# Where one block sum is made: GpSimd in place of VectorE for product 7 of a seven-product matmul group

## The chip, the core and the metric

One core of a Trainium2 chip runs the whole program. The metric is device time in microseconds (us) for one execution: the kernel before took 1982.58 us in the median of 3 runs (1981.91 to 1983.2).

## The reference, cut to what matters

One decoder layer on 256 tokens of width 2048, in float32: a half-step SwiGLU feed-forward, a two-branch attention mixer, and a second half-step feed-forward, with layer norms between them.

```python
def _swiglu(x, w_gate, w_up, w_down):
    return (jax.nn.silu(x @ w_gate) * (x @ w_up)) @ w_down
...
h = _layer_norm(ALPHA * h + 0.5 * _swiglu(h, ffn1...), ...)
mix = _mixer(h, positions, w_in, ...)          # gates, q/k/v projections, attention, w_out
h = _layer_norm(ALPHA * h + mix, ...)
h = _layer_norm(ALPHA * h + 0.5 * _swiglu(h, ffn2...), ...)
```

The change touches matmuls of the 256 x 2048 activations by weight columns: gate and up of both feed-forwards (2048 x 5632 each), and gates and differential-attention projections of the mixer.

## The kernel before, in words

**A product of two float32 numbers in three matmuls.** Every operand is split into a rounded part and a rest. `split` (L148 to L150) makes the rounded part with a cast on ScalarE (ACT in the profile, L149) and the rest with a subtraction on VectorE (DVE, L150). `triple` (L201 to L204) then issues three matmuls on TensorE (PE): high by high (L202), high by low (L203), low by high (L204). So the two weight halves of a pair are first needed one matmul apart.

**Units and their ring.** Work on the weights goes in units of one 128x1024 tile: `load` starts a DMA on SyncE's queue, `prep` casts and subtracts into a pair of tiles from a ring (`wring`, six pairs in the groups), `now` issues the matmuls. `look(3, 4)` keeps three loaded and four prepared units ahead of the matmuls. The framework then lays out each engine's queue by priority and by when it takes an operand to be ready, so an instruction can stand earlier in its engine's queue than in the code; each engine works through its queue in order.

**A group (`Hybrid.group`, L310).** Two 512-column blocks of weights are multiplied together. For part of the depth, seven products of sums and differences stand in for eight plain ones; the rest is done plainly (`plain`, L361). The sums on the weights' side are made in place in `seventh.prep` (L341 to L347), one per half `s`: for product 5, block 11 becomes 11+12; for 6 it becomes 11+12+22; for 7, block 12 becomes 12+22; for 4, block 11 takes 21. All of these are the additions of L344. They read and write the raw weight tiles (`sraw`), which the loads of the next group overwrite when the last reader is done.

```python
plan = {1: ("11", "11", None, "X"), 5: ("12", "11", ("11", "12"), "Z"), 6: ("22", "11", ("11", "22"), "X"),
        7: (None, "12", ("12", "22"), "X"), 2: ("21", "21", None, "Y"), 4: (None, "11", ("11", "21"), "W"),
        3: (None, "22", None, "Z")}
```

The order of units is 1, 1, plain, 5, 5, plain, 6, 6, plain, 7, 7, plain and so on to product 3, with one plain unit more at the end: 14 units of six matmuls and 8 of twelve, 180 matmuls. After products 1, 5, 6 and 7 ScalarE copies a bank (L321, L322).

**Where groups run.** Each feed-forward runs ten groups (L772), the mixer six (L1011, L1020, L1026): 26 groups. A feed-forward group ends in `sum_done` (L726): VectorE adds bank and copy (`gus`, L728), ScalarE takes the silu (L715), VectorE multiplies (`hb`, L719) and transposes (`blocks`, L606), and GpSimd issues eight DMAs that store the transposed tile (`hT`, L608). In the groups GpSimd (POOL) has only such DMA issues to do.

Of the kernel before, what the change touches and what calls it, by code (L numbers as in the profile page):

```python
# [15 lines left out]
ALU = mybir.AluOpType  # L16
# [43 lines left out]
def layer_kernel(ctx: ExitStack, tc: tile.TileContext, a: dict, out: bass.AP):  # L60
    nc = tc.nc
    V, S, GP, PE = nc.vector, nc.scalar, nc.gpsimd, nc.tensor
# [9 lines left out]
    def nm(s):  # L72
        uid[0] += 1
        return f"{s}_{uid[0]}"
# [10 lines left out]
    def mm_bank(name="mm"):  # L85
        return psum.tile([P, 512], F32, tag="mm", name=nm(name), bufs=5)
# [61 lines left out]
    def split(hi, lo, src):  # L148
        S.copy(hi, src)  # L149
        V.tensor_tensor(out=lo, in0=src, in1=hi.bitcast(F32), op=ALU.subtract)  # L150
# [12 lines left out]
    def catch_up(n):  # L163
        while len(behind) > n:
            behind.popleft()()
# [22 lines left out]
    def unit(load, prep, now, later_on=None):  # L188
        if load is not None:
            load()  # L190
        loaded.append((prep, now, later_on))
        advance(*ahead)

    def next_pair():
        assert len(ring) > len(prepared) + lag[0], (len(ring), len(prepared), lag[0])
        catch_up(len(ring) - 1)
        pair = ring.pop(0)
        ring.append(pair)
        return pair

    def triple(o, xh, xl, wh, wl, first, last, again=False):  # L201
        PE.matmul(o, xh, wh, start=first, stop=False, skip_group_check=again)  # L202
        PE.matmul(o, xh, wl, start=False, stop=False, skip_group_check=again)  # L203
        PE.matmul(o, xl, wh, start=False, stop=last, skip_group_check=again)  # L204
# [93 lines left out]
    class Hybrid:  # L298
# [11 lines left out]
        def group(self, w0, w1, done):  # L310
            banks = {}
            snap = [t[:, i, :] for t in self.snaps[self.turn % len(self.snaps)] for i in range(2)]
            self.turn += 1
            n1, n2, n3, q5 = snap
            R = self.raws
            blocks = {"11": (w0, 0), "12": (w1, 0), "21": (w0, 2), "22": (w1, 2)}
# [4 lines that stand above are left out]
            after = {1: lambda: S.copy(n1, banks["X"]), 6: lambda: S.copy(n2, banks["X"]),  # L321
                     7: lambda: S.copy(n3, banks["X"]), 5: lambda: S.copy(q5, banks["Z"]),  # L322
                     2: lambda: done(0, 0, banks["Y"], n1, ALU.subtract),
                     4: lambda: done(0, 1, banks["W"], n3, ALU.subtract)}
            stops = {1, 5, 6, 7, 2, 4}

            def bank(n):
                first = n not in banks
                if first:
                    banks[n] = mm_bank()  # L330
                return banks[n], first

            def seventh(p, s):
                load_block, src, add, b = plan[p]
                st = {}

                def load():
                    w, j0 = blocks[load_block]
                    nc.sync.dma_start(R[load_block][s], w[j0 + s])

                def prep():  # L341
                    t = R[src][s]
                    if add is not None:
                        V.tensor_tensor(out=t, in0=t, in1=R[add[1]][s], op=ALU.add)  # L344
                    pair = next_pair()
                    split(*pair, t)
                    st["pair"] = [v.rearrange("p (g n) -> p g n", g=G) for v in pair]  # L347

                def now():
                    o, first = bank(b)  # L350
                    wh, wl = st["pair"]
                    xh, xl = self.seven.at_[p]
                    for g in range(G):
                        k = 2 * s + g
                        triple(o, xh[:, k, :], xl[:, k, :], wh[:, g, :], wl[:, g, :], first and g == 0,
                               s == 1 and g == 1 and p in stops, b in "XZ")
                    if s == 1 and p in after:
                        after[p]()
                unit(load if load_block else None, prep, now)

            def plain(n, j, last=False):  # L361
                w = (w0, w1)[n]
                names = (("Y", "W"), ("Z", "X"))[n]
                st = {}

                def load():
                    st["raw"] = wpool.tile([P, 1024], F32, tag="raw", name=nm("raw"), bufs=4)
                    nc.sync.dma_start(st["raw"], w[j])

                def prep():  # L370
                    pair = next_pair()
                    split(*pair, st["raw"])
                    st["pair"] = [v.rearrange("p (g n) -> p g n", g=G) for v in pair]

                def now():
                    wh, wl = st["pair"]
                    for b in range(2):
                        o, first = bank(names[b])
                        for g in range(G):
                            k = 2 * j + g  # L380
                            triple(o, self.x.at(0, k, b), self.x.at(1, k, b), wh[:, g, :], wl[:, g, :],
                                   first and g == 0, last and g == 1, n == 1)
                    if last:
                        done(1, 0, banks["Z"], n2, ALU.add)
                        done(1, 1, banks["X"], q5, ALU.add)
                unit(load, prep, now)

            end = self.k_tiles // G - 1
            for p, n, j in zip((1, 5, 6, 7) + self.last, (0, 0, 0, 0, 1, 1, 1), (4, 5, 6, 7, 4, 5, 6)):
                for s in range(2):  # L390
                    seventh(p, s)
                plain(n, j)
            plain(1, end, True)
# [927 lines left out]
```

## Time and profile before

| what | time |
|---|---|
| median of 3 runs | 1982.58 us (1981.91 to 1983.2) |
| the profiled execution: span from its first to its last instruction | 1981.9 us |
| TensorE busy in it | 1967.9 us (99%) |
| VectorE busy | 1770.4 us (89%) |
| ScalarE busy | 1247.6 us (63%) |
| GpSimd busy | 248.8 us (13%) |

Of the profiled execution the record gives the span and no time beside it. The median is 0.7 us above that span, which is as much as can lie around it. A row of the timeline gives start and length of an instruction; consecutive ones of a line are merged (x3). On VectorE the next instruction starts some 0.08 us before the one ahead of it has ended, so what an instruction costs its engine is the distance from start to start.

### The profile page before, as it was taken

The page shows a single profiled execution, that of the slowest core. Times are in us where ns is not written, and L with a number is a line of the kernel's source. Part 1 is how long each engine was busy: PE and PEld are TensorE (multiplying, and loading weights), DVE is VectorE, ACT ScalarE, POOL GpSimd, SP SyncE. Part 2 cuts the span into 40 slices and gives each one's busy share as a digit, 9 for nine tenths or more (in the row PEclk, how much of TensorE's full clock was granted, in tenths as well). Part 3 has the DMA queues.
Part 4 walks back from the last instruction along what each step waited for, and adds up shares of the span by engine and source line. Part 5 has one row for each costly group of instructions (what it writes and reads, how often), then busy time and mean ns, then how long its engine had stood idle before and what let it go on. Part 6 is the DMA issues. An engine that isn't in the chain of part 4 may idle for free.

```text
span 1981.9 us, 25344 instructions
## 1 busy us (share of the span) xinstructions
PE 1967.9 (99%) x8832; PEld 1628.9 (82%) x8832; DVE 1770.4 (89%) x2089; ACT 1247.6 (63%) x1571; POOL 248.8 (13%) x463
## 2 busy tenths in 40 slices
PE   9999999999999999999999999999999999999997
PEld 7888888888888888888888888888888888888886
DVE  7999999999799889999877676799999999998986
ACT  6666666666556566666667764566666666665552
POOL 0111101012010011002223130001011100121000
PEclk9999999999999999999999999999999999999999
DMA  8667766658678666677667667657676666596763
GB/s 323 220 212 237 262 211 202 218 199 313 232 228 274 204 221 246 220 245 250 228 215 249 228 225 264 220 208 242 225 257 229 201 216 228 186 327 225 256 222 125
DMA packets 133649, 460.50 MB, mean 232 GB/s; under 512 B 19424, under 2 KB 19472, under 8 KB 133520
## 3 DMA queue, kind: packets, MB, share of 16 engines
q1 hardware_dynamic: 109296, 389.59, 57.4%
q0 software_dynamic: 24224, 69.29, 11.2%
q8 instruction: 69, 1.13, 0.2%
q14 instruction: 60, 0.49, 0.1%
HBM read 429.97 MB, written 28.84 MB: 231 GB/s over the span
## 4 chain that ended last, share of the span: by engine, by line
PE 90%; DVE 4%; DMA 3%; issue 2%; ACT 1%; SPq 0%; POOL 0%; DVEq 0%; ACTq 0%; POOLq 0%
PE mm L203 29%; PE mm L204 29%; PE mm L202 29%; DVE wring L150 2%; DMA raw<-in_dn_dram 1%; PE tr L203 1%; PE tr L204 1%; PE tr L202 1%; ACT wring L149 1%; DVE sraw L344 0%; PE tr L571 0%; DMA hraw<-hT 0%; DMA raw<-in_wgd_dram 0%; DMA raw<-in_gu_dram 0%; DVE sraw L519 0%
## 5 line engine op out<-in xcount | busy, mean ns | idle before, releaser
L149 ACT CAST wring<-raw 128x1024 fp32r<-128x1024 f32 (+2 forms) x499 | 516.2, 1039 | 338.7 <-PE mm L204 236.6
L150 DVE TENSOR_TENSOR wring<-raw,wring 128x1024 fp32r<-128x1024 f32 (+2 forms) x499 | 596.7, 1202 | 117.0 <-ACT wring L149 110.3
L149 ACT CAST wring<-sraw 128x1024 fp32r<-128x1024 f32 x436 | 453.7, 1052 | 217.4 <-PE mm L204 98.1
L150 DVE TENSOR_TENSOR wring<-sraw,wring 128x1024 fp32r<-128x1024 f32 x436 | 523.6, 1217 | 35.2 <-ACT wring L149 31.0
L204 PE MATMUL mm<-wring,h 128*128 128x512 f32 (+2 forms) x1296 | 499.3, 386 | 0.0
L203 PE MATMUL mm<-wring,h 128*128 128x512 f32 (+2 forms) x1296 | 498.5, 385 | 0.3 <-DVE wring L150 0.3
L202 PE MATMUL mm<-wring,h 128*128 128x512 f32 (+2 forms) x1296 | 498.6, 385 | 0.0
L203 PE MATMUL mm<-wring,xs 128*128 128x512 f32 x776 | 302.3, 390 | 0.3 <-DVE wring L150 0.3
L202 PE MATMUL mm<-wring,xs 128*128 128x512 f32 x776 | 302.5, 390 | 0.0
L204 PE MATMUL mm<-wring,xs 128*128 128x512 f32 x776 | 302.1, 389 | 0.0
L204 PEld LDWEIGHTS mm<-wring,h 128*128 128x128 f32 x1296 | 243.5, 188 | 48.9 <-DVE h L150 1.4
L202 PEld LDWEIGHTS mm<-wring,h 128*128 128x128 f32 x1296 | 243.5, 188 | 48.8 <-ACT h L149 1.0
L203 PEld LDWEIGHTS mm<-wring,h 128*128 128x128 f32 x1296 | 243.5, 188 | 48.7 <-DVE wring L150 0.9
L344 DVE TENSOR_TENSOR sraw<-sraw,sraw 128x1024 f32<-128x1024 f32 x208 | 249.9, 1211 | 1.6 <-DMA sraw<-in_gu_dram 1.5
L608 POOL DMA_DIRECT2D hT<-blocks x176 | 95.7, 551 | 766.5 <-DVE blocks L606 711.5
L203 PEld LDWEIGHTS mm<-wring,xs 128*128 128x128 f32 x776 | 145.7, 188 | 31.5 <-DVE wring L150 1.6
L202 PEld LDWEIGHTS mm<-wring,xs 128*128 128x128 f32 x776 | 145.7, 188 | 31.1 <-ACT snap L321 0.7
L204 PEld LDWEIGHTS mm<-wring,xs 128*128 128x128 f32 x776 | 145.7, 188 | 30.1
L203 PE MATMUL mm<-wring,x 128*128 128x512 f32 x384 | 149.6, 390 | 0.6 <-DVE wring L150 0.6
L202 PE MATMUL mm<-wring,x 128*128 128x512 f32 x384 | 149.5, 390 | 0.3 <-ACT wring L149 0.3
L204 PE MATMUL mm<-wring,x 128*128 128x512 f32 x384 | 149.3, 389 | 0.0
L203 PEld LDWEIGHTS mm<-wring,x 128*128 128x128 f32 x384 | 72.1, 188 | 16.2 <-DVE wring L150 1.3
(268 smaller groups left out, 1921.2 us busy)
## 6 DMA issues: line engine op xcount, KB each, us to landing
raw<-in_gu_dram SPq DMA_DIRECT2D x191, 512.0 KB, 4.4
sraw<-in_gu_dram SPq DMA_DIRECT2D x160, 512.0 KB, 5.2
raw<-in_dn_dram SPq DMA_DIRECT2D x140, 512.0 KB, 4.6
sraw<-in_dn_dram SPq DMA_DIRECT2D x36, 512.0 KB, 5.3
hraw<-hT POOLq DMA_DIRECT2D x68, 256.0 KB, 5.7
raw<-in_w_out_dram SPq DMA_DIRECT2D x32, 512.0 KB, 4.4
raw<-in_wgd_dram SPq DMA_DIRECT2D x24, 512.0 KB, 4.6
hT<-blocks POOLq DMA_DIRECT2D x176, 64.0 KB, 2.3
```

The costliest lines, as they stand in the source:

```text
L149: S.copy(hi, src)
L150: V.tensor_tensor(out=lo, in0=src, in1=hi.bitcast(F32), op=ALU.subtract)
L202: PE.matmul(o, xh, wh, start=first, stop=False, skip_group_check=again)
L203: PE.matmul(o, xh, wl, start=False, stop=False, skip_group_check=again)
L204: PE.matmul(o, xl, wh, start=False, stop=last, skip_group_check=again)
L344: V.tensor_tensor(out=t, in0=t, in1=R[add[1]][s], op=ALU.add)
L608: nc.gpsimd.dma_start(to.rearrange("(g r) (i f) -> i r g f", g=4, i=4)[i], t[32 * i:32 * (i + 1), :].rearrange("r (g f) -> r g f", g=4))
```

## The change

In `seventh.prep`, the addition for product 7 is no longer issued on VectorE. When product 6 of the same half is prepared, GpSimd is given the same addition, 12 += 22, behind VectorE's addition for product 6. Product 7's cast and subtraction then read the tile that GpSimd wrote. Tiles, loads, matmuls and all other additions stay as they are.

```diff
@@ -340,8 +340,10 @@
 
                 def prep():
                     t = R[src][s]
-                    if add is not None:
+                    if add is not None and p != 7:
                         V.tensor_tensor(out=t, in0=t, in1=R[add[1]][s], op=ALU.add)
+                    if p == 6:
+                        GP.tensor_tensor(out=R["12"][s], in0=R["12"][s], in1=R["22"][s], op=ALU.add)
                     pair = next_pair()
                     split(*pair, t)
                     st["pair"] = [v.rearrange("p (g n) -> p g n", g=G) for v in pair]
```

## The prediction

> **What bounds the kernel now.** I read the page first, then who waited for whom on TensorE, then busy time by stretches of one group's length, then the timeline of one group on VectorE, TensorE and GpSimd.
>
> ```profile
> span 1981.9 us, 25344 instructions
> PE 1967.9 (99%) x8832; PEld 1628.9 (82%) x8832; DVE 1770.4 (89%) x2089; ACT 1247.6 (63%) x1571; POOL 248.8 (13%) x463
> PE 90%; DVE 4%; DMA 3%; issue 2%; ACT 1%; SPq 0%; POOL 0%; DVEq 0%; ACTq 0%; POOLq 0%
> ```
>
> TensorE is busy for 99% of the span and makes up 90% of the chain that ends last. Its waits in the whole run are these:
>
> ```profile
> PE mm L203 <- DVE wring L150: 1.2, 4, 0.4
> PE tr L98 <- DVE zero L96: 1.1, 1, 1.1
> PE tr L203 <- DVE wring L150: 0.3, 1, 0.3
> PE mm L202 <- ACT wring L149: 0.3, 1, 0.3
> ```
>
> The columns are total us, times, longest. TensorE waited for prepared weights for 1.2 + 0.3 + 0.3 = 1.8 us in all. So nothing that relieves VectorE can be worth more than about **1.8 us**, under 0.1%. But VectorE is not far from becoming the bound itself. By stretches of a group's length (for each engine busy us and instructions; then clock, DMA share, GB/s), two in the feed-forwards and the six in the mixer:
>
> ```profile
> 255.90:296.70 40.80, 40.80 (x181) 33.78 (x180) 39.55 (x41) 26.39 (x31) 4.35 (x8) 1.00 0.65 219
> 1617.40:1658.20 40.80, 40.80 (x181) 33.79 (x181) 39.54 (x41) 26.38 (x31) 4.33 (x8) 1.00 0.65 219
> 746.00:787.00 41.00, 40.89 (x182) 33.09 (x182) 39.32 (x56) 25.50 (x33) 5.45 (x10) 1.00 0.73 256
> 787.00:828.00 41.00, 40.70 (x180) 33.30 (x179) 38.07 (x36) 24.82 (x26) 2.17 (x4) 1.00 0.63 222
> 828.00:869.00 41.00, 41.00 (x183) 33.95 (x182) 38.55 (x36) 24.81 (x26) 2.16 (x4) 1.00 0.69 233
> 869.00:910.00 41.00, 41.00 (x183) 33.95 (x182) 37.46 (x37) 24.70 (x26) 5.26 (x10) 1.00 0.71 234
> 910.00:951.00 41.00, 41.00 (x183) 33.95 (x182) 38.32 (x38) 26.25 (x30) 10.10 (x20) 1.00 0.78 248
> 951.00:992.00 41.00, 41.00 (x181) 33.66 (x180) 37.15 (x37) 27.90 (x34) 9.80 (x18) 1.00 0.69 226
> ```
>
> A feed-forward group takes 40.80 us, all of it TensorE at a granted clock of 1.00; VectorE, the third pair of numbers, is busy for 39.55 of them. Its spare time is **1.25 us a group**. In the mixer it has 1.7 to 3.9. GpSimd, the fifth pair, is nearly free.
>
> **What is removed.** The timeline of VectorE in the group whose matmuls begin at 255.90:
>
> ```profile
> 248.22 1.22 DVE L344 TENSOR_TENSOR sraw<-sraw,sraw 128x1024 f32<-128x1024 f32 x1
> 249.36 1.21 DVE L150 TENSOR_TENSOR wring<-sraw,wring 128x1024 fp32r<-128x1024 f32 x1
> ...
> 253.90 1.22 DVE L344 TENSOR_TENSOR sraw<-sraw,sraw 128x1024 f32<-128x1024 f32 x1
> 255.03 0.68 DVE L728 TENSOR_TENSOR gus<-mm,snap 128x512 f32<-128x512 f32 x1
> 255.63 1.21 DVE L150 TENSOR_TENSOR wring<-sraw,wring 128x1024 fp32r<-128x1024 f32 x1
> ...
> 263.83 3.49 DVE L150 TENSOR_TENSOR wring<-sraw,wring 128x1024 fp32r<-128x1024 f32 x3
> 267.23 1.22 DVE L344 TENSOR_TENSOR sraw<-sraw,sraw 128x1024 f32<-128x1024 f32 x1
> ...
> 269.50 3.54 DVE L150 TENSOR_TENSOR wring<-sraw,wring 128x1024 fp32r<-128x1024 f32 x3
> ```
>
> Of the eight additions of L344 in the group, I take those at 253.90 and 267.23 for the two halves of product 7, by their place in the queue: the one at 248.22 is product 5's first. From start to start such an addition costs VectorE 249.36 - 248.22 = 1.14 us. Two go per group, 52 in 26 groups: 52 x 1.14 = 59 us of VectorE. On the path they are worth at most the 1.8 us above, because TensorE hides them; I count nothing.
>
> **What is added: the length of one sum on GpSimd.** The trace has no GpSimd addition. Its nearest rows:
>
> ```profile
> L608 POOL DMA_DIRECT2D hT<-blocks x176 | 95.7, 551 | 766.5 <-DVE blocks L606 711.5 <-DVE hb L719 52.5 <-issue 2.5
> L842 POOL TENSOR_SCALAR_AFFINE_SELECT mask<-mask 128x128 f32<-128x128 f32 x2 | 0.5, 287 | 0.0
> L840 POOL MEMSET mask<- 128x384 f32 x1 | 0.4, 422 | 0.0
> masks.py:197 POOL MEMSET ident<- 128x128 f32 x1 | 0.2, 204 | 0.3 <-POOLq L1305 0.3
> ```
>
> From below: the fill, which only writes, costs (422 - 204) / 256 = 0.85 ns an element, so 1024 take some 1.0 us. From above: the select reads one input and writes, 287 ns for 128 elements; eight of that size are 2.30 us, and if each of two inputs cost that much, 4.6. I take **2.3 us**, since the select is the nearest row and its start-up, counted eight times there, leaves room for the second input. [...]
>
> **What it takes from VectorE.** This is the unknown that decides. Call it b: the time by which one GpSimd sum holds VectorE up. No row shows GpSimd reading a tile while VectorE works; its DMA issues beside VectorE (0.55 us each) read none. So b lies between 0 (they run side by side) and 4.6 (VectorE stands still for the longest sum). I take b = 2.3, the whole length of one sum, for this reason: both engines would stream whole tiles at once, and between ends that far apart it is the middle and the one length that a row gives. [...]
>
> **What is queued behind it.** GpSimd's sum needs blocks 12 and 22 loaded and product 5's addition of the same half done. In the shown group VectorE made the sum at 253.90 without a wait, and product 5's first addition ended at 248.22 + 1.22 = 249.44, so GpSimd can start the first between 249.4 and 253.9, the second soon after. Behind VectorE's held instruction stand the subtractions for products 5, 6 and 7, and behind those TensorE:
>
> ```profile
> 266.79 0.39 PE L202 MATMUL mm<-wring,xs 128*128 128x512 f32 x1
> 267.02 0.39 PE L203 MATMUL mm<-wring,xs 128*128 128x512 f32 x1
> ...
> 273.59 0.39 PE L202 MATMUL mm<-wring,xs 128*128 128x512 f32 x1
> 273.82 0.39 PE L203 MATMUL mm<-wring,xs 128*128 128x512 f32 x1
> ```
>
> The L203 at 267.02 is the first to need product 6's subtraction, the first of the three at 263.83, done at 265.05: a margin of 1.97 us. The one at 273.82 needs the second half of product 7, the middle one of the three from 269.50, done at about 271.86: again 1.96. Three readings of the loss per feed-forward group, with b = 2.3:
>
> - Both sums ahead of product 6's subtraction: 2 x 2.3, less the one addition removed ahead of it (1.14), less the margin: 4.6 - 1.14 - 1.97 = 1.49.
> - Only one ahead of it: no loss there (2.3 - 3.11 is negative); at product 7, with two additions gone, 4.6 - 2.28 - 1.96 = 0.36.
> - VectorE's budget over the whole group: 39.55 - 2.28 + 4.6 = 41.87, which is 1.07 over TensorE's 40.80.
>
> I take the last, which lies between the other two and is what a steady run of groups cannot escape: 20 groups x 1.07 = 21.4 us. In the mixer the same budget adds 2.32 to 39.32, 38.07, 38.55, 37.46, 38.32 and 37.15 against 41.0; only the first exceeds it, by 0.64. Sum: **22.0 us**. On the profiled execution's span that is 1981.9 + 22.0 = 2003.9; the median of the runs is 0.7 above the span, and 1982.58 + 22.0 = **2004.6 us**.
>
> **Costed at nothing.** On GpSimd's own queue stand the eight DMA issues of the group:
>
> ```profile
> 260.16 4.35 POOL L608 DMA_DIRECT2D hT<-blocks  x8 [32.34 <-DVE blocks L606]
> ```
>
> ScalarE's casts of such blocks, in the list of groups:
>
> ```profile
> L149 ACT CAST wring<-sraw 128x1024 fp32r<-128x1024 f32 x436 | 453.7, 1052 | 217.4 <-PE mm L204 98.1
> ```
>
> The issues start after 32 us of idleness, so two sums of 2.3 us fit ahead. Should the sums stand behind the issues, the first would be done at 264.51 + 2.3 = 266.8 and the second at 269.1; product 7's second half then needs a cast (1.05 us) and a subtraction (1.22) before 273.82, so until 271.5 there is room. If the sums delay the stores, these have tens of us before they are read. The loads that overwrite blocks 12 and 22 wait for products 7 and 3, which stand later than the sum. SyncE's queue issues the same loads.
>
> **The rivals.**
>
> - *They run side by side (not slower).* The place is product 6's subtraction, the price 2b - 3.11, and it decides below b = 1.55, where nothing is lost: 2b fits into the removed addition and the margin. For it: b may be as low as 0, and TensorE's matmuls hide VectorE's work in every group now. Against it: VectorE has 1.25 us to spare. Time: 1982.6, at best 1.8 less.
> - *GpSimd waits for VectorE.* VectorE's queue is dense, and a sum may have to wait for a row like `gus` at 255.03, 0.60 us from start to start, before it runs; then VectorE is held for 2.3 - 0.6 = 1.7 instead of 2.3. Loss at product 6: 3.4 - 3.11 = 0.29, 20 x 0.29 = 5.8 us, 1988.4. If the sum never got a turn before product 7 needs it, TensorE would wait for many us a group; the idle time on VectorE speaks against that.
> - *A sum is longer than 2.3.* At b = 3.4, half way to the upper end, product 6 costs 6.8 - 3.11 = 3.69 a group, 74 us in 20 groups, and the mixer's budget some 10 more: 2066.
>
> The queues may also be laid out differently once 52 additions have left VectorE's. TensorE's longest wait for weights is now 0.4 us, so one such shift is worth little either way, and I give it no case beyond a small chance of a gain.
>
> **How the numbers follow.** If b is spread evenly from 0 to 4.6, it lies above the threshold of 1.55 in two cases of three. The chances: the forecast 0.45; side by side 0.25; GpSimd waits 0.15, of which a fifth stays within 0.2%; longer sums 0.12; a gain 0.03. 0.2%, some 4 us, is about what a measurement of this kernel can tell from no change. So slower is 0.45 + 0.12 + 0.12 = 0.69, within 0.2% 0.25 + 0.03 = 0.28, faster 0.03. As the case of no change cannot be left out, the range begins at 1982.58 - 1.8 = 1980.8. It ends where b = 2.75: 20 x (5.5 - 3.11) = 48, 2030. Longer sums are left out. The forecast's own range is 1989.9 (20 x 0.36) to 2030.
>
> **What would show it.** Right: additions on POOL of some 2.3 us, 52 of them; VectorE instructions that last 2 us and more beside them; TensorE waiting at L203 for L150 once a group, 1 to 1.5 us, and groups of about 41.9 us. Wrong: groups still at 40.80 with VectorE's rows unchanged at 1.22 (side by side); groups near 41.1 with POOL's additions lying in VectorE's one-input rows (GpSimd waits); additions of 3 us and more. A stall of a kind that is not in these groups, in the down projections for instance, would make the reasoning wrong even where the sum is right.

## The result and the profile after

| | before | after |
|---|---|---|
| median of 4 runs | 1982.89 us (1981.91 to 1983.8) | 2074.04 us (2070.79 to 2079.53) |
| ratio with its 95% interval | 1 | 1.0462 [1.0449, 1.0475] |
| span of the profiled execution | 1981.9 us | 2073.5 us |
| mean granted TensorE clock in it | 0.998 | 0.984 |

The change costs 91 us. The forecast had the sign; 2074 lies far above its range.

The page of the kernel after, its head and two groups of instructions:

```profile
span 2073.5 us, 25509 instructions
PE 2006.0 (97%) x8832; PEld 1644.6 (79%) x8832; DVE 1819.1 (88%) x2037; ACT 1240.1 (60%) x1571; POOL 413.0 (20%) x515
L346 POOL TENSOR_TENSOR sraw<-sraw,sraw 128x1024 f32<-128x1024 f32 x52 | 163.5, 3145 | 556.8 <-DVE sraw L344 480.5
L344 DVE TENSOR_TENSOR sraw<-sraw,sraw 128x1024 f32<-128x1024 f32 x156 | 236.6, 1518 | 12.7 <-DMA sraw<-in_wdq_dram 3.4
```

VectorE issues 52 instructions fewer and yet is busy for 1819.1 us instead of 1770.4: 52 x 1.14 = 59 us left it, and some 108 us came. They come as waiting inside its rows. The durations (min/median/max ns) by line:

```profile
L346 POOL TENSOR_TENSOR sraw<-sraw,sraw x52: 2361/3312/3381, 46.4 to 1784.1; 128x1024 f32<-128x1024 f32 x52
```

```profile
L344 DVE TENSOR_TENSOR sraw<-sraw,sraw x156: 1180/1212/3307, 43.4 to 1806.3; 128x1024 f32<-128x1024 f32 x156
```

The shortest GpSimd addition takes 2.36 us, most take 3.31; a VectorE addition mostly takes 1.21, but up to 3.31 when a GpSimd addition lies beside it. How the two meet is seen in the timelines of one group, GpSimd first, then VectorE:

```profile
261.96 3.31 POOL L346 TENSOR_TENSOR sraw<-sraw,sraw 128x1024 f32<-128x1024 f32 x1 [19.73 <-DVE sraw L344]
267.57 3.31 POOL L346 TENSOR_TENSOR sraw<-sraw,sraw 128x1024 f32<-128x1024 f32 x1 [2.30 <-DVE sraw L344]
```

```profile
261.79 1.22 DVE L150 TENSOR_TENSOR wring<-sraw,wring 128x1024 fp32r<-128x1024 f32 x1
262.93 3.42 DVE L150 TENSOR_TENSOR wring<-raw,wring 128x1024 fp32r<-128x1024 f32 x1
266.28 1.21 DVE L344 TENSOR_TENSOR sraw<-sraw,sraw 128x1024 f32<-128x1024 f32 x1
267.41 1.21 DVE L150 TENSOR_TENSOR wring<-sraw,wring 128x1024 fp32r<-128x1024 f32 x1
268.66 3.30 DVE L344 TENSOR_TENSOR sraw<-sraw,sraw 128x1024 f32<-128x1024 f32 x1
271.88 0.68 DVE L730 TENSOR_TENSOR gus<-mm,snap 128x512 f32<-128x512 f32 x1
...
280.62 1.21 DVE L344 TENSOR_TENSOR sraw<-sraw,sraw 128x1024 f32<-128x1024 f32 x1
281.75 3.48 DVE L150 TENSOR_TENSOR wring<-sraw,wring 128x1024 fp32r<-128x1024 f32 x3
```

The sum starts at 261.96 while VectorE's row of 261.79 runs, and ends at 265.27; the VectorE row behind that one starts at 262.93 and ends only at 266.35, 1.1 us after the sum. So the sum first lets the running row finish (3.31 instead of 2.36), and then the next row stands still until the sum is through: from start to start it costs 266.28 - 262.93 = 3.35 us, 2.21 more than 1.14. The second sum does the same to the addition at 268.66 (271.88 - 268.66 = 3.22, 2.08 more). Ten us later product 6's second subtraction is late. It is the first of the three at 281.75; the addition at 280.62, ahead of it, is product 4's. TensorE's rows there, with the idle time before one in brackets:

```profile
280.70 0.50 PE L202 MATMUL mm<-wring,xs 128*128 128x512 f32 x1
283.02 0.50 PE L203 MATMUL mm<-wring,xs 128*128 128x512 f32 x1 [1.81 <-DVE wring L150]
...
284.98 0.63 PE L203 MATMUL mm<-wring,x 128*128 128x512 f32 x1
285.41 0.63 PE L204 MATMUL mm<-wring,x 128*128 128x512 f32 x1
```

The L203 should have started 0.23 us behind the L202, at 280.93; it started at 283.02, 2.09 us late. Soon behind the stall, in the last two rows, the matmuls come every 0.43 us instead of every 0.23: the clock granted to TensorE there is 0.51 (the stretch from 283.90 below). Busy time of the engines by stretches (us and instructions; clock, DMA share, GB/s last), two whole groups and then the stall's stretch and the next two:

```profile
187.30:232.00 44.70, 42.88 (x181) 34.92 (x180) 41.67 (x39) 25.90 (x31) 12.12 (x12) 0.96 0.63 212
232.00:275.10 43.10, 41.28 (x181) 33.70 (x181) 42.48 (x41) 27.80 (x35) 13.22 (x14) 1.00 0.66 232
...
280.50:283.90 3.40, 1.59 (x7) 0.94 (x6) 3.40 (x4) 3.40 (x5) 0.89 (x2) 1.00 0.75 213
283.90:287.40 3.50, 3.50 (x10) 2.75 (x9) 3.50 (x4) 1.60 (x3) 0.00 (x0) 0.51 0.67 176
287.40:290.80 3.40, 3.40 (x16) 2.80 (x16) 3.27 (x4) 1.68 (x2) 0.00 (x0) 1.00 0.86 304
```

A group without the half clock takes 43.1 us, 2.3 more than before; one with it takes 44.7. A gap of 1.81 us, in a stretch in which TensorE was busy for 1.59 of 3.40 us, was followed by 3.5 us at 0.51: ten matmuls were done in them, where the next stretch did sixteen. Thirteen feed-forward groups and three places in the mixer have such a stretch of 3.4 us (one of them twice that).

Why thirteen of twenty, when nearly all have the same stall? In the trace's clock records these half-clock stretches last 3.413 us (that one 6.827) and begin whole multiples of 3.413 us apart: 195.198 and 283.944, for one, are 26 of them apart. What tells the stalls of this run apart is how they fall into steps of that length, counted from those beginnings. The step ahead of a half-clock stretch, and one with a stall of the same length that has none behind it:

```profile
147.40:150.80 3.40, 1.58 (x7) 0.81 (x6) 3.40 (x4) 3.40 (x5) 1.34 (x3) 1.00 0.77 212
413.70:417.10 3.40, 1.74 (x7) 0.94 (x5) 3.40 (x4) 3.27 (x4) 1.90 (x4) 1.00 0.71 172
```

In the feed-forward groups all thirteen steps in which TensorE was busy for 1.6 us or less were followed by half clock; where a stall was spread over two steps and the emptier one still had 1.74 us or more, none was. This is read off one run; no run varied it alone. Over the run the clock fell from 0.998 to 0.984: 0.014 x 2073.5 = 29 us. TensorE's waits, the two largest (us in total, times, longest):

```profile
PE mm L203 <- DVE wring L150: 43.5, 28, 2.8
PE mm L202 <- ACT snap L321: 5.9, 3, 2.3
```

So the 91 us are some 29 of half clock and 62 of stalls, which stand in these waits, in smaller ones and, as in the group above, partly in the rows around them. Both kernels issue the same 8832 matmuls in nearly the same order, so that the nth of one can be set against the nth of the other: 31 us are lost in the groups of the first feed-forward, 26 in the mixer's and 36 in those of the second.

### The profile page after: what moved, and what is told of

Same layout as the page of the kernel before. It is cut to its first block, busy times and chain, and to the rows that moved or that the text cites. A ratio compares the mean times of both kernels' runs of the same rounds, so it can differ in the third digit from the quotient of the medians.

```text
span 2073.5 us, 25509 instructions
## 1 busy us (share of the span) xinstructions
PE 2006.0 (97%) x8832; PEld 1644.6 (79%) x8832; DVE 1819.1 (88%) x2037; ACT 1240.1 (60%) x1571; POOL 413.0 (20%) x515
## 4 chain that ended last, share of the span: by engine, by line
PE 85%; DVE 7%; issue 4%; DMA 3%; ACT 1%; DVEq 0%; SPq 0%; ACTq 0%
PE mm L203 27%; PE mm L204 27%; PE mm L202 27%; DVE wring L150 4%; DVE sraw L344 1%; ACT wring L149 1%; PE tr L204 1%; PE tr L203 1%; PE tr L202 1%; DMA sraw<-in_wdq_dram 1%; DMA turned<-turn 1%; PE tr L573 0%; DMA sraw<-in_wgm_dram 0%; DMA sraw<-in_wdk_dram 0%; DMA raw<-in_wc_dram 0%
## 5 line engine op out<-in xcount | busy, mean ns | idle before, releaser
L150 DVE TENSOR_TENSOR wring<-raw,wring 128x1024 fp32r<-128x1024 f32 (+2 forms) x499 | 646.2, 1301 | 136.5 <-ACT wring L149 130.4
L150 DVE TENSOR_TENSOR wring<-sraw,wring 128x1024 fp32r<-128x1024 f32 x436 | 529.8, 1228 | 44.3 <-ACT wring L149 37.7
L203 PE MATMUL mm<-wring,h 128*128 128x512 f32 (+2 forms) x1296 | 502.9, 388 | 5.1 <-DVE wring L150 5.1
L202 PE MATMUL mm<-wring,h 128*128 128x512 f32 (+2 forms) x1296 | 503.0, 388 | 0.0
L204 PE MATMUL mm<-wring,h 128*128 128x512 f32 (+2 forms) x1296 | 502.6, 388 | 0.0
L203 PE MATMUL mm<-wring,xs 128*128 128x512 f32 x776 | 309.4, 399 | 37.7 <-DVE wring L150 37.7
L202 PE MATMUL mm<-wring,xs 128*128 128x512 f32 x776 | 308.3, 397 | 7.9 <-ACT snap L321 5.9
L204 PE MATMUL mm<-wring,xs 128*128 128x512 f32 x776 | 307.8, 397 | 0.0
L203 PEld LDWEIGHTS mm<-wring,h 128*128 128x128 f32 x1296 | 246.2, 190 | 56.4 <-DVE wring L150 7.3
L202 PEld LDWEIGHTS mm<-wring,h 128*128 128x128 f32 x1296 | 246.4, 190 | 50.0 <-ACT h L149 1.0
L204 PEld LDWEIGHTS mm<-wring,h 128*128 128x128 f32 x1296 | 245.8, 190 | 49.8 <-DVE h L150 1.4
L346 POOL TENSOR_TENSOR sraw<-sraw,sraw 128x1024 f32<-128x1024 f32 x52 | 163.5, 3145 | 556.8 <-DVE sraw L344 480.5
L344 DVE TENSOR_TENSOR sraw<-sraw,sraw 128x1024 f32<-128x1024 f32 x156 | 236.6, 1518 | 12.7 <-DMA sraw<-in_wdq_dram 3.4
L203 PEld LDWEIGHTS mm<-wring,xs 128*128 128x128 f32 x776 | 147.9, 191 | 75.3 <-DVE wring L150 45.5
L202 PEld LDWEIGHTS mm<-wring,xs 128*128 128x128 f32 x776 | 147.2, 190 | 46.6 <-ACT wring L149 9.0
L204 PEld LDWEIGHTS mm<-wring,xs 128*128 128x128 f32 x776 | 148.4, 191 | 30.2
L202 PE MATMUL mm<-wring,x 128*128 128x512 f32 x384 | 152.2, 397 | 0.8 <-ACT wring L149 0.8
L203 PE MATMUL mm<-wring,x 128*128 128x512 f32 x384 | 151.8, 395 | 0.7 <-DVE wring L150 0.7
L204 PE MATMUL mm<-wring,x 128*128 128x512 f32 x384 | 151.1, 394 | 0.0
```

The lines of the kernel that those rows point to most:

```text
L346: GP.tensor_tensor(out=R["12"][s], in0=R["12"][s], in1=R["22"][s], op=ALU.add)
```

## The experiments

Theory A, formed from this trace: a GpSimd sum **holds** VectorE up by 2.2 us (b), and what counts is less VectorE's budget over the group than the lead of the next subtraction that TensorE needs. For product 6's second subtraction, before: the three from 263.83 end at 267.32, the second of them one pitch (1.14) earlier at 266.18, and TensorE's row for it is

```profile
268.38 0.39 PE L203 MATMUL mm<-wring,xs 128*128 128x512 f32 x1
```

That is a lead of 2.20 us. After: two holds (2.21 + 2.08), less the removed addition (1.14), plus product 4's addition that the layout put ahead of it (1.14), less the lead: 2.09 us, the measured stall. Theory B: the new order of VectorE's queue alone is late. Theory C: product 7 waits for its sum on the slower engine. Ratios are against the kernel before, run on the same chip (1983.1, 1982.6 and 1983.3 us).

### The order without the sum: no_sum

```diff
 if add is not None and p != 7:
     V.tensor_tensor(...)
-if p == 6:
-    GP.tensor_tensor(out=R["12"][s], ...)
```

> Leaves out the sum for product 7 altogether (neither VectorE nor GpSimd makes it, so product 7 uses block 12 alone); all else, VectorE's queue order too, is as in the changed kernel. Theory 1 (a GpSimd sum holds VectorE, 2.2 us each by the rows of 3.4 instead of 1.2 us beside it): with no GpSimd sums nothing is held, TensorE is the bound again, 1981 to 1985 us. Theory 2 (the other order of VectorE's queue, with product 4's addition ahead of product 6's second subtraction, is what costs): the loss stays, 2030 us or more.

Measured: 1982.13 us, 0.9995 [0.9986, 1.0004]. VectorE's queue is that of the kernel after, product 4's addition (264.00) ahead of product 6's second subtraction (the first of three at 265.13), and TensorE does not wait:

```profile
264.00 1.22 DVE L344 TENSOR_TENSOR sraw<-sraw,sraw 128x1024 f32<-128x1024 f32 x1
265.13 3.49 DVE L150 TENSOR_TENSOR wring<-sraw,wring 128x1024 fp32r<-128x1024 f32 x3
```

```profile
PE mm L203 <- DVE wring L150: 1.7, 4, 0.6
```

B falls. It also shows the most that any way of making this sum elsewhere can bring, at no cost at all: nothing that can be measured.

### The sum without the relief: extra_add

The kernel before, whole, with an added GpSimd sum of the same size whose result nothing uses.

```diff
+spare = const.tile([P, 1024], F32, name="spare")
...
+if p == 6:
+    GP.tensor_tensor(out=spare, in0=spare, in1=R["22"][s], op=ALU.add)
```

> The kernel before with VectorE's sums and queue as they were, and beside them two GpSimd additions a group on a spare tile that nobody waits for (spare += block 22). Theory 1: VectorE is held 2 x 2.2 us a group and gains nothing back; at product 6's first subtraction 4.4 - 1.97 = 2.4 us of stall a group, so as slow as the changed kernel or slower, 2070 to 2110 us. Theory 2, and a third one (product 7 waits for its late sum): 1981 to 1986 us.

Measured: 2074.0 us, 1.0462 [1.0447, 1.0476], the ratio of the change itself, at clock 0.985.

```profile
L348 POOL TENSOR_TENSOR spare<-spare,sraw 128x1024 f32<-128x1024 f32 x52 | 160.8, 3093 | 543.8 <-DMA sraw<-in_gu_dram 443.9 <-DMA sraw<-in_wgm_dram 35.4 <-DMA sraw<-in_wdq_dram 18.6
```

```profile
PE mm L205 <- DVE wring L152: 42.8, 28, 1.8
```

Nothing waits for this sum's result, so C falls. The same loss comes with all additions still on VectorE, and a stall of the same length:

```profile
283.82 0.39 PE L206 MATMUL mm<-wring,x 128*128 128x512 f32 x1
284.39 0.50 PE L204 MATMUL mm<-wring,xs 128*128 128x512 f32 x1 [0.18 <-ACT wring L151]
286.71 0.79 PE L205 MATMUL mm<-wring,xs 128*128 128x512 f32 x1 [1.82 <-DVE wring L152]
```

```profile
285.45 3.48 DVE L152 TENSOR_TENSOR wring<-sraw,wring 128x1024 fp32r<-128x1024 f32 x3
```

286.71 - 284.39 - 0.23 = 2.09. But it stands at another place. The L204 at 284.39 is the first row behind a plain unit, so it opens product 6's first half, and it is the first of the three subtractions, done at 286.66, that it waited for. The lead there was 1.97 in the kernel before, VectorE's order is the same as before, and A gives 4.29 - 1.97 = 2.32, which is 0.23 too much; why is not settled. That the stall is as long as in the change, where the second half waits, is chance. So is the equal total, for a second thing differs. The group, from copy to copy, is

```profile
240.41:285.37 44.96, 42.96 (x180) 34.84 (x180) 44.83 (x43) 28.06 (x36) 12.38 (x15) 0.96 0.66 223
```

VectorE is full here (44.83 of 44.96), so its budget would lengthen these groups even without the stall. In the changed kernel VectorE has room again, and the stall is no shorter for it.

### GpSimd busy, but reading nothing: extra_fill

The kernel before, with three GpSimd fills of 128x1024 at the same place, into `spare` as in extra_add (ScalarE first writes one column, which ties them to it).

```diff
+if p == 6:
+    S.copy(spare[:, 0:1], R["22"][s][:, 0:1])
+    for _ in range(3):
+        GP.memset(spare, 0.0)
```

> As extra_add, but each GpSimd addition is replaced by three fills of the spare tile, which write 128x1024 and read nothing, about 1 us each (and one column copied by ScalarE ties them to block 22). Theory 1 in the form that only GpSimd's reading holds VectorE: no VectorE row over 1.25 us beside the fills, 1981 to 1987 us. If any GpSimd work on tiles holds VectorE: 2 x 3 us a group, over 2090 us.

Measured: 1983.0 us, 0.9998 [0.999, 1.0007]. The fills are there, 0.96 us each, three times as many as the sums, and VectorE's additions are never longer than 1.23 us:

```profile
L350 POOL MEMSET spare<- 128x1024 f32 x156 | 149.2, 957 | 570.3 <-ACT spare L348 564.3
```

```profile
L346 DVE TENSOR_TENSOR sraw<-sraw,sraw x208: 1177/1216/1227, 42.6 to 1717.3; 128x1024 f32<-128x1024 f32 x104
```

GpSimd's being at work on fills was harmless here; its reading, in the changed kernel, was not: there such an addition took up to 3.31 us.

### One sum of the two: one_half

```diff
-if add is not None and p != 7:
+if add is not None and (p != 7 or s == 1):
...
-if p == 6:
+if p == 6 and s == 0:
```

> Only the first half's sum for product 7 goes to GpSimd; the second half's stays on VectorE: 26 GpSimd sums instead of 52. Theory 1 with its margin: one hold of 2.2 us less one removed addition of 1.14 is 1.1, under the 1.97 us of margin, so no stall in the feed-forward groups, 1981 to 1990 us (some loss in the mixer possible). A fixed price per GpSimd sum (91 us / 52 = 1.75 us): 1983 + 26 x 1.75 = 2028 us.

Measured: 2004.49 us, 1.011 [1.0096, 1.0123]. TensorE at product 6's first half, in one group:

```profile
309.88 0.39 PE L202 MATMUL mm<-wring,xs 128*128 128x512 f32 x1
310.32 0.50 PE L203 MATMUL mm<-wring,xs 128*128 128x512 f32 x1
```

The expectation by A, 1981 to 1990, missed, though the halved change costs a quarter, not half, as a lead that has to be used up first would have it. It counted the removed addition as time won ahead of the subtraction; in the trace the other half's addition had moved up into that place (299.19). So one hold of 2.2 stands against the first half's lead of 1.97, and the L203 is 310.32 - 309.88 - 0.23 = 0.21 us late. That explains the feed-forwards only, and they are the smaller part: set matmul against matmul, their groups lose 9 of the 21 us and the mixer's six lose 10.5, which the expectation had left open.

### Half the length: half_cols

GpSimd adds columns 0 to 511, VectorE the rest in its old place.

```diff
-V.tensor_tensor(out=t, in0=t, in1=R[add[1]][s], op=ALU.add)
+c = slice(512, 1024) if p == 7 else slice(0, 1024)
+V.tensor_tensor(out=t[:, c], in0=t[:, c], in1=R[add[1]][s][:, c], op=ALU.add)
+if p == 6:
+    GP.tensor_tensor(out=R["12"][s][:, 0:512], in0=R["12"][s][:, 0:512], in1=R["22"][s][:, 0:512], op=ALU.add)
```

> GpSimd adds 512 of the 1024 columns of each half, VectorE the other 512: 52 GpSimd sums of half the length. Theory 1 (hold as long as the sum): about 1.2 us a sum and 1.1 held; with the queue as it comes out, 2.3 held + 0.6 + 1.14 moved ahead - 1.14 removed = 2.9 against 2.2 of margin at product 6's second subtraction: 0.7 us a group, 14 us in the feed-forwards and up to half of 29 in the mixer, 1990 to 2015 us. A fixed price per GpSimd instruction: 2074 us.

Measured: 2000.8 us, 1.0088 [1.0073, 1.0103], clock 0.998.

```profile
L150 DVE TENSOR_TENSOR wring<-raw,wring x499: 674/1222/2329, 4.8 to 1968.2; 128x1024 fp32r<-128x1024 f32 x161, 128x512 fp32r<-128x512 f32 x3, 128x640 fp32r<-128x640 f32 x3
```

The longest held subtraction is 2.33 us: 1.11 over its own 1.22, where the whole sum held it for 2.2. The hold goes with the length of the sum; a fixed price for each meeting, which would have kept 2074, falls. The time lies in what was expected by A; set matmul against matmul, the feed-forwards' groups lose 13 us, where A gave 14, and the mixer's 5.

### A reader with one input: extra_copy

The kernel before, with `GP.tensor_copy(spare, R["22"][s])` in the place of extra_add's sum.

> The kernel before with two GpSimd copies a group of block 22 into a spare tile: one input read, 128x1024, nothing removed from VectorE. Theory 1 (whoever reads holds the other out for its whole length): VectorE rows beside it lengthened by the copy's own length; at 1.0 to 1.3 us a copy two holds of 2.0 to 2.6 against a margin of 1.97 us cost 0 to 0.6 us a group, 1982 to 2000 us. If only two-input GpSimd instructions hold VectorE: rows of 1.22 us throughout, 1983 us.

Measured: 1993.12 us, 1.0048 [1.0032, 1.0065].

```profile
L346 DVE TENSOR_TENSOR sraw<-sraw,sraw x208: 1174/1217/2069, 42.9 to 1731.4; 128x1024 f32<-128x1024 f32 x104
```

One tile read is enough for a hold, 2.07 - 1.22 = 0.85 us here. Two of them, 1.7 us, are under the leads of 1.97 and 2.20, and yet 10 us are lost. Set matmul against matmul, the twenty feed-forward groups lose only 4 of them, 0.2 a group, nearly as A has it; 4 are lost in the mixer and 2.5 between the first feed-forward's groups and the mixer. What loses them there wasn't followed.

### The old order with the sum: queue_kept

The kernel after, but product 4's addition and product 7's subtractions may not be laid ahead of product 6's subtraction of the second half.

```diff
...
+with tc.issue_after(rest[0].ins) if p == 4 else ExitStack():
     V.tensor_tensor(out=t, in0=t, in1=R[add[1]][s], op=ALU.add)
...
+with tc.issue_after(rest[0].ins) if p == 7 else ExitStack():
+    made = split(*pair, t)
+if p == 6:
+    rest[:] = [made]
```

> The changed kernel, with VectorE's queue held to the order of before around product 6: the subtractions for product 7 and the additions for product 4 are issued behind product 6's second subtraction. Theory A (the loss is hold minus margin, and the planner's new order, with product 4's addition put ahead of that subtraction, took 1.14 us of the margin): the stall in a feed-forward group falls from 2.1 to about 0.95 us, and without stalls of 2 us the clock may stay at 1.0: 20 groups x 0.95 = 19 us plus 0 to 29 us in the mixer, 2002 to 2031 us. Theory B (order is of no account, each GpSimd sum costs its 1.75 us): 2074 us.

Measured: 2032.2 us, 1.0254 [1.0239, 1.0269], 42 us less than the change. A group, and TensorE's rows at product 6's second half in it:

```profile
225.40:267.50 42.10, 41.34 (x182) 33.75 (x181) 41.52 (x41) 27.17 (x35) 16.65 (x14) 1.00 0.68 238
```

```profile
230.97 0.50 PE L202 MATMUL mm<-wring,xs 128*128 128x512 f32 x1
232.24 0.50 PE L203 MATMUL mm<-wring,xs 128*128 128x512 f32 x1 [0.76 <-DVE wring L150]
```

The L203 is 232.24 - 230.97 - 0.23 = 1.04 us late, where A gave 4.29 - 1.14 - 2.20 = 0.95. The group loses 42.10 - 40.80 = 1.30 us instead of 2.3, and with this stall the clock stays at 1.00. Only the last group of each feed-forward still stalls for over 2 us, and the clock over the run is 0.996, against 0.984. The upper end of the expected range, 2031, is just passed. So the layout's one shift costs 1 us a group directly and most of the half clock besides.

### One more instruction out of the way: queue_better

As queue_kept, and the plain unit's subtraction ahead of product 6's second one is held back too (`issue_after` around the `split` in `plain` for that unit).

> As queue_kept, and the subtraction of the plain unit behind product 6 is issued behind product 6's second subtraction too, another 1.14 us earlier. Theory A: no stall at product 6; what is left is VectorE's budget, 39.05 us from start to start before, less 2.27, plus 4.4 held: 41.2 against 40.8, 8 us in 20 groups, plus 0 to 29 in the mixer: 1990 to 2020 us, under queue_kept in any case. Theory B: 2074 us.

Measured: 2033.08 us, 1.0256 [1.0241, 1.0271]. The expectation, under queue_kept, missed. VectorE's rows at the place:

```profile
272.58 1.21 DVE L346 TENSOR_TENSOR sraw<-sraw,sraw 128x1024 f32<-128x1024 f32 x1
274.90 1.23 DVE L150 TENSOR_TENSOR wring<-sraw,wring 128x1024 fp32r<-128x1024 f32 x1 [1.11 <-ACT wring L149]
```

With nothing between, product 6's addition, its cast on ScalarE and its subtraction follow each other directly, and VectorE stands idle for 1.11 us until the cast is done. The plain subtraction had filled just that time.

### The stall filled with matmuls: fill_stall

The kernel after, with nine matmuls that nothing uses ahead of product 6's second half in each feed-forward group: 180 x 0.227 = 41 us of TensorE's work added.

```diff
+if p == 6 and s == 1 and len(self.snaps) == 2:
+    extra = tr_bank("extra")
+    for _ in range(9):
+        PE.matmul(extra, xh[:, 2, :], wh[:, 0, :], start=True, stop=True)
```

> The changed kernel with work added: in feed-forward groups TensorE repeats one matmul nine times (9 x 0.227 = 2.0 us, into a bank that nobody reads) right ahead of the one that waits for product 6's second subtraction. Theory C (half-clock stretches of 3.4 us that follow the stalls are a part of the loss of their own, 13 of them in the feed-forwards, 47.8 us at half speed, so 24 us): TensorE is not idle, the clock stays at 1.0, and the kernel gets faster by being given more to do, 2045 to 2058 us. If the clock is no cost: 2074 us or more.

Measured: 2051.01 us, 1.0349 [1.0334, 1.0365], as expected: with 41 us more to do it is **23 us faster** than the change. A group:

```profile
317.60:360.80 43.20, 43.20 (x191) 35.39 (x190) 41.52 (x39) 26.01 (x32) 10.96 (x10) 1.00 0.62 207
```

TensorE is busy throughout, the clock is 1.00, and the group takes 43.2 us, the change's 43.1 without its half-clock stretches. The clock over the run is 0.996, against the change's 0.984: it was the stall that the half clock followed, not the load of work.

### By stage: ffn_only and mixer_only

The change in the feed-forwards' twenty groups alone, and in the mixer's six alone.

```diff
+small = len(self.snaps) == 1
-if add is not None and p != 7:
+if add is not None and (p != 7 or small):
...
-if p == 6:
+if p == 6 and not small:
```

> GpSimd makes product 7's sums in the 20 feed-forward groups alone; the six mixer groups are as before. From the stages of the changed kernel (30 us later by the end of the first feed-forward's groups, 29 in the mixer, 33 in the second): about 1983 + 63 = 2040 to 2050 us.

> GpSimd makes product 7's sums in the six mixer groups alone. If the loss there is made in the mixer itself (loads that start late behind late subtractions), 1983 + 29 = 2005 to 2016 us. If the mixer only pays for arriving late or at a lower clock from the feed-forward ahead of it: 1983 to 1990 us.

Measured: 2049.2 us, 1.0336 [1.032, 1.0351], at clock 0.988; and 2006.14 us, 1.0115 [1.0098, 1.0132], at 0.996. Both lie within what was expected. So the feed-forwards lose 65.9 us and the mixer 22.9; 88.8 together against the change's 91.2. Of the 65.9 the half clock makes 0.010 x 2047.1 = 20 us; the other 45 are 20 x 2.3, the groups' lengthening at full clock. In the mixer the waits between 740 and 1000 us before, and between 740 and 1025 in mixer_only:

```profile
ACT wring L149 <- DVE sraw L344: 22.1, 22, 4.7
```

```profile
ACT wring L149 <- DVE sraw L345: 43.3, 18, 6.8
...
PE mm L203 <- DVE wring L150: 7.5, 8, 2.5
...
PE tr L914 <- DVE kr_row L909: 3.9, 2, 2.7
```

ScalarE's casts wait twice as long for VectorE's additions there, in fewer and longer pieces. TensorE waits for weights, but also for `kr_row`, a small row that VectorE makes in its turn, so part of the loss is not at the place of the sum. Besides, the kernel keeps blocks 12 and 21 of the mixer in one tile (L305), so that there the load of 21 waits for product 7's readers within the same group, and not only the next group's loads. What makes six groups lose 23 us, 3.8 each, where twenty lose 3.3 each, is not settled: that loads into tiles which late subtractions still read come late in their turn is argued, not shown.

## Why the prediction was wrong

**Bound, and nothing to be won: right.** "I count nothing" for the 59 us taken off VectorE; no_sum shows 0.9995 with the sum left out altogether.

**Length of a sum, 2.3 us: right, with some luck.** The shortest in the trace is 2.36. The forecast had it from another instruction with one input, and guessed that its start-up would pay for the second.

**b = 2.3 between 0 and 4.6: right.** Measured 2.08 to 2.21. In the trace the waiting goes in both directions: the sum waits for the running row (3.31 us for 2.36), and the next VectorE row for the sum (3.42 for 1.21); beside fills, which read nothing, no addition took over 1.23. Not every row was held: in the mixer of the kernel after, two rows that read a bank and two transposes run beside a sum at 0.6 us each, as `gus` rows do elsewhere (0.60 from start to start):

```profile
959.54 2.57 POOL L346 TENSOR_TENSOR sraw<-sraw,sraw 128x1024 f32<-128x1024 f32 x1
```

```profile
959.77 1.27 DVE L1020 TENSOR_TENSOR dqTr<-mm,snap 128x512 f32<-128x512 f32 x2
960.97 1.29 DVE L608 STREAM_TRANSPOSE blocks<-dqTr 128x512 f32<-128x512 f32 x2
```

**The reading of the three: wrong.** The forecast chose VectorE's budget, 41.87 us a group, 1.07 over TensorE's. The budget came out right (41.67 and 42.48 in the two groups shown, 41.52 in fill_stall's), but it is only a lower bound, and the groups take 43.1: VectorE's work is there, but not at the place where TensorE needs it. What decides is the lead at product 6, which the forecast's first reading priced at 1.49, for the first half. That reading counted the removed addition, 1.14, as won. In the forecast's words: "The queues may also be laid out differently once 52 additions have left VectorE's ... one such shift is worth little either way". That sentence is the **step that failed**. The layout filled the freed place with product 4's addition, ahead of product 6's second subtraction: with it the stall is 2.09 us and a half-clock stretch mostly follows, without it (queue_kept) the stall is 1.04 and mostly none does. That is 2074.04 - 2032.2 = 42 of the 69 us that the forecast missed; most of the others are the mixer's. No_sum shows why the sentence looked safe: with the lead whole, the same shift costs nothing.

**Clock at 1.00: not seen as a term.** The profile before has it at 1.00 in every group, and the sum had no line for it. It makes 29 of the 91 us.

**The mixer at 0.6 us: wrong.** Budgets as an average said that five of six groups have room; the mixer alone loses 22.9. No row of the mixer was read for a lead, as was done for the feed-forward; whether leads would have given the 22.9 is not shown, and the cause there stays open.

So the forecast's 22.0 = 21.4 + 0.6 stands against about 45 (feed-forwards at full clock), 20 to 25 (half clock there) and 23 (mixer). A slip of 0.1 in its own lower end (1982.58 + 20 x 0.36 is 1989.8, not 1989.9) changes nothing. Of the rivals, side by side fell with b; GpSimd waits for VectorE came in part, but the hold behind it stayed whole; a longer sum did not come. Of the signs, those of "right" came in kind (52 additions, VectorE's rows of over 2 us, L203 waiting for L150 once a group), but with other amounts: stalls of 2.1 instead of 1 to 1.5, groups of 43.1 and 44.7 instead of 41.9. A sign of "wrong", additions of 3 us and more, came as well, and misled: a row of 3.31 is 2.36 of its own and a wait for VectorE's running row.

## What to carry to other kernels

Before moving work from a busy engine to an idle one, read whether the bound engine waits for the busy one at all; if it does not, the move can only cost. What it costs is at least what the busy engine's budget lacks, and beyond that it was decided here at one place, in the feed-forward groups: the lead of the next operand that the bound engine needs, against all that the move puts ahead of it, with each freed slot counted as filled by whatever the framework can lay there. And a stall of about 2 us on TensorE is to be priced with the half-clock stretch that may follow it, here 1.7 us more each in thirteen groups of twenty.

## What the runs showed of the hardware

- A GpSimd row that read a tile and a VectorE row with two tile inputs held each other up in the meetings shown: 3.31 us for a sum of 2.36, and 3.42 us for a VectorE row of 1.21 beside it (after), 2.33 for one of 1.22 beside a sum of half the length (half_cols), 2.07 beside a copy (extra_copy); beside fills, 1.23 at most (extra_fill). Two rows that read a bank passed beside a sum in 1.27 us together, two transposes in 1.29 (after, from 959.77).
- A stall of 1.04 us left the clock at 1.00 in the group shown (queue_kept); stalls of 2.1 us or somewhat more were followed in 13 groups of 20 by 3.4 us at about 0.5 (after), those in which TensorE was busy for 1.6 us or less of one step of 3.413 us; and 41 us of matmuls that nothing uses made the kernel 23 us faster (fill_stall).
- A GpSimd fill of 128x1024 took 0.96 us (extra_fill), the shortest sum of two tiles 2.36 (after).
